# A hybrid encoder layer: the bias table resident, separate buffers for even heads, another layout of v, and smaller rings

## The chip, the cores and the metric

The kernel runs on one core of a Trainium2 chip. The metric is the device time of one execution in microseconds, lower is better, given as the median of several runs. A core has a matrix engine (TensorE; its weight loads are listed apart), VectorE, ScalarE, GpSimd, and a queue engine, SyncE, that here issues nearly all DMAs. On-chip memory (SBUF) has 128 partitions; matmul results land in PSUM banks. Everything else lies in DRAM and comes by DMA.

## The reference

One layer over a sequence of 2048 positions with 1024 channels, in float32, then a final RMSNorm:

```
hn = rmsnorm(x, norm_g)
z  = hn @ w_in                      # one projection, split among three groups of heads
A) attention, 6 heads of 64: scores = q k^T / 8 + rel_bias[clip(distance)], softmax, times v
   over a band of chunks of 64 (own chunk and 8 before); gated by silu(ag)
B) mLSTM, 6 heads of 64: causal conv of width 4 and silu on q and k, chunkwise matrix memory
C) gated linear attention (GLA), 4 heads: chunkwise state with a decay per key channel
out = rmsnorm(x + concat(yA, yB, yC) @ w_out, final_g)
```

The relative bias differs from a constant only in the last 256 key positions of a query tile of 128; the kernel subtracts the constant of far distances and so needs a table of 128 x 6 x 256 for the six heads.

## The kernel before

**Two parts.** The first (from `with ExitStack() as pa_`, line 145) runs four blocks of 512 positions. A block makes all projections, with the mLSTM and GLA work of the block interleaved, and stores what attention needs in DRAM: q (`q_d`), k (`k_d`), v (`v_d`), the gate (`ga_d`), and the finished mLSTM and GLA outputs (`y_d`). The second part (from line 983) loads these, head by head, does attention and the output projection. Six projections of the last block, all for attention, are held back (`kept`) and run as filler between the score steps of attention for block 0 (`proj_kept`, `attention0`, lines 1259 to 1263).

**Precision.** Operands are split in a high and a low part (float32r), and a product takes three matmuls: high x high, high x low, low x high (lines 241 to 243). A weight tile is loaded in `wraw`, its high part cast by ScalarE (line 232), its low part made by VectorE or GpSimd (line 233), into a tile `w` of the ring `wring`, six buffers of 8 KB a partition. A feature projection uses one `w`, and a token projection (`proj_t`, v and part of GLA) holds four through its four position tiles. The second part takes five buffers of the same ring for w_out (line 1025).

**The conv.** `proj_m` runs six projections. Each is copied from its PSUM bank to a tile `u` (ScalarE, line 579); a scale (line 586) and three multiply-adds on VectorE (line 588) read it. `u` has two buffers; the projections use two PSUM banks `ip`. In the last block a tile `u` also holds two GLA outputs (line 911).

**The bias.** `bias_rel` (line 641) runs in the last block: it loads the far constant and, in three pieces, the table, adds the negated constant on ScalarE (line 649), sets masked entries on GpSimd (line 650) and stores the piece in DRAM, `b_d`. The second part loads all of it to `bt` (line 996), 768 KB. VectorE reads `bt` when it takes scores from PSUM (line 1094).

**Heads.** `scores(q, h)` (line 1054) loads for one head of one block the query halves `qq` (two DMAs), the keys `kk` and the values `vv`, the first two from a pool `early` with two buffers each, which lies in the part of SBUF (`side="right"`) that the first part's pools used. It yields between score steps: six for block 0, eight later. `mix(q, h)` transposes the softmax weights, splits them (`ph` on ScalarE, `pl` on VectorE, lines 1144 and 1145) and multiplies by `vv` (lines 1154 and 1157). `attention0` runs heads 0 and 1 with score steps alone, and from head 2 on merges the scores of head h with the mix of head h - 2. `load_wo` (line 1006) loads and splits w_out and the outputs of the first part meanwhile.

**What sets the order.** TensorE runs in program order (`manual_schedule`, line 135). The other engines' and SyncE's orders come from a planner that simulates the program: it takes what is ready by program order, with `high_priority` ahead, and gives buffers out as they come free. `flow` (line 35) decides by estimated times where the mLSTM and GLA steps stand between the projections.

Of the kernel before, what the change touches and what calls it, by code (L numbers as in the profile page):

```python
# [8 lines left out]
FP32 = mybir.dt.float32  # L9
# [7 lines left out]
P = 128  # L17
# [88 lines left out]
def trunk_kernel(ctx: ExitStack, tc: tile.TileContext, xT, x, w_f, w_t, w_o, w_gates, norm_g, conv_w,  # L106
# [9 lines left out]
    v_d = dram.tile([AH, S, P], FP32, name="v_d")  # L116
# [3 lines left out]
    b_d = dram.tile([P, AH, 256], FP32, name="b_d")  # L120

# [19 lines left out]
    wring = pg_.enter_context(tc.tile_pool(name="wring", bufs=6))  # L141
# [3 lines left out]
    with ExitStack() as pa_:  # L145
# [381 lines left out]
        def proj_v(X):  # L527
            vg = big.tile([P, NC, 256], FP32, name="vg", bufs=1)
            vs = []

            def evac1(tt, ps):
                v = ev.tile([P, AH, 2, 64], FR, name="hl")
                v5 = v.rearrange("p (a b) l d -> p a b l d", b=2)
                pv4 = ps[:, 0:384].rearrange("p (a b d) -> p a b d", b=2, d=64)
                nc.scalar.copy(vg[:, tt, P:2 * P], ps[:, 384:512])
                for b in range(2):
                    nc.scalar.copy(v5[:, :, b, b, :], pv4[:, :, b, :])
                    nc.vector.tensor_tensor(v5[:, :, b, 1 - b, :], pv4[:, :, b, :], f32(v5[:, :, b, b, :]), op=ALU.subtract)
                t0 = st["q"] * QT + tt * P
                nc.sync.dma_start(v_d[:, t0:t0 + P, :].rearrange("h t d -> t h d"), f32(v).rearrange("p h l d -> p h (l d)"))  # L540

            def evac0(tt, ps):
                v = big.tile([P, 6, 65], FP32, name="v", bufs=NC)
                vs.append(v)
                nc.scalar.activation(v[:, :, 0:64], ps[:, 0:384].rearrange("p (h d) -> p h d", h=6), AF.Copy, scale=1.0 / 32)
                nc.gpsimd.memset(v[:, :, 64:65], 1.0 / 32)
                nc.scalar.copy(vg[:, tt, 0:P], ps[:, 384:512])  # L547

            proj_t(0, X, evac0)
            yield vs, vg  # L550
            proj_t(1, X, evac1)
            yield
# [19 lines left out]
        def proj_m(X):  # L572
            qk = big.tile([P, 6, QT], FP32, name="qk", bufs=1)
            tail = big.tile([P, 6, 3], FP32, name="tail")
            for b in range(6):
                ps = proj_f(("mq" if b < 3 else "mk") + str(b % 3), X)
                zb = big.tile([P, 3 + QT], FP32, name="u", bufs=2)
# [63 lines left out]
        def bias_rel():  # L641
            bc = big.tile([P, AH], FP32, name="sm")
            nc.sync.dma_start(bc, bias[:, :, 256])
            nc.vector.tensor_scalar(bc, bc, -1.0, None, op0=ALU.mult)
            for p in range(AH // 2):
                b2 = g_tile([P, QT]).rearrange("p (h j) -> p h j", h=2)
                nc.sync.dma_start(b2, bias[:, 2 * p:2 * p + 2, 0:256])
                for h in range(2):
                    nc.scalar.activation(b2[:, h, :], b2[:, h, :], AF.Identity, bias=bc[:, 2 * p + h:2 * p + h + 1])
                nc.gpsimd.memset(b2[0:64, :, 192:256], NEG)  # L650
                nc.sync.dma_start(b_d[:, 2 * p:2 * p + 2, :], b2)
# [191 lines left out]
        def gla(q, vg, gg, G, held=None):  # L843
            for sub in range(2):
# [7 lines left out]
                for c in range(2):  # L852
# [54 lines left out]
                    if held is not None:  # L907
                        if not held:
                            ocs = rows
                        elif len(held) == 2:  # L910
                            ocs = big.tile([P, 3 + QT], FP32, name="u", bufs=2)
# [22 lines left out]
        for q in range(NQ):  # L934
# [3 lines left out]
            if q == NQ - 1:  # L938
# [9 lines left out]
                bias_rel()  # L948
# [21 lines left out]
            flow.need("gates")  # L970
            M = dict(R)
# [12 lines left out]
    with ExitStack() as pb_:  # L984
        psum = pb_.enter_context(tc.tile_pool(name="psumb", bufs=2, space=PSUM, reuse_waits="tile"))
        early = pb_.enter_context(tc.tile_pool(name="early", bufs=2, side="right", reuse_waits="tile"))
# [8 lines left out]
        bt = one.tile([P, AH, 256], FP32, name="bt", bufs=1)  # L995
        nc.sync.dma_start(bt, b_d)
# [57 lines left out]
        def scores(q, h, out_):  # L1054
# [3 lines left out]
            qq = early.tile([P, 2, QT], FR, name="qq")  # L1058
# [4 lines left out]
            kk = early.tile([P, 1024], FR, name="kk")  # L1063
            dma.dma_start(f32(kk[:, :nk]), k_d[h, :, :, kb:kb + nk].rearrange("l d t -> (l d) t"))
            vv = big.tile([P, 8, P], FR, name="vv", bufs=3)
            dma.dma_start(f32(vv[:, :nk // P, :]), v_d[h, kb:kb + nk, :].rearrange("(b p) d -> p b d", p=P))
# [300 lines left out]
```

## Time and profile before

| | |
|---|---|
| runs | median 1308.42 us of 3 (1305.0 to 1312.47) |
| profiled execution | 1308.93 us, of which the span of instructions 1307.2 us |
| mean granted TensorE clock | 0.984 |
| busy | TensorE 1267.8 us, weight loads 1035.1, VectorE 807.6, GpSimd 601.4, ScalarE 592.2 |
| DMA | 179.53 MB in 105937 packets, 137 GB/s on average |

The first part's blocks take about 280, 235, 230 and 162 us; the second part begins at about 907 us. Matmuls are pipelined, so the length of one in the timeline (0.39 us for 128x512) is not its cost: in a row they start 0.23 us apart. A row of the timeline has start, length, engine, line, operation, output and inputs, and in brackets the idle time before it with what ended it. `PEclk` in a table of stretches is the clock that TensorE was granted, 1.00 being full speed. In the list of DMA issues the last number is the median time from issue to landing.

### The profile page before, as it was taken

The page shows a single profiled execution, that of the slowest core. Times are in us where ns is not written, and L with a number is a line of the kernel's source. Part 1 is how long each engine was busy: PE and PEld are TensorE (multiplying, and loading weights), DVE is VectorE, ACT ScalarE, POOL GpSimd, SP SyncE. Part 2 cuts the span into 40 slices and gives each one's busy share as a digit, 9 for nine tenths or more (in the row PEclk, how much of TensorE's full clock was granted, in tenths as well). Part 3 has the DMA queues.
Part 4 walks back from the last instruction along what each step waited for, and adds up shares of the span by engine and source line. Part 5 has one row for each costly group of instructions (what it writes and reads, how often), then busy time and mean ns, then how long its engine had stood idle before and what let it go on. Part 6 is the DMA issues. An engine that isn't in the chain of part 4 may idle for free.

```text
span 1307.2 us, 19535 instructions
## 1 busy us (share of the span) xinstructions
PE 1267.8 (97%) x6924; PEld 1035.1 (79%) x6924; DVE 807.6 (62%) x1866; ACT 592.2 (45%) x1098; POOL 601.4 (46%) x829
## 2 busy tenths in 40 slices
PE   9999999999999999999999999998989989999997
PEld 7777878887787887877778787887777878878876
DVE  6837656762767677276566765653467667666631
ACT  5636322643532246353224643332466556655631
POOL 3337742333765224376523555643164444554432
PEclk8999999999999999998999999999989999999999
DMA  5256234324522442462344332327686565655322
GB/s 201 60 163 228 70 123 135 104 87 148 207 69 94 137 132 57 152 216 85 91 131 123 104 126 64 120 70 234 191 232 212 172 190 160 187 172 180 97 90 80
DMA packets 105937, 179.53 MB, mean 137 GB/s; under 512 B 9712, under 2 KB 54640, under 8 KB 105840
## 3 DMA queue, kind: packets, MB, share of 16 engines
q1 hardware_dynamic: 101376, 170.16, 42.3%
q10 hardware_dynamic: 4464, 8.13, 1.7%
q8 instruction: 54, 0.88, 0.3%
q14 instruction: 43, 0.35, 0.1%
HBM read 141.83 MB, written 36.44 MB: 136 GB/s over the span
## 4 chain that ended last, share of the span: by engine, by line
PE 76%; DVE 7%; POOL 5%; ACT 4%; DMA 4%; issue 3%; SPq 0%; POOLq 0%; ACTq 0%; DVEq 0%
PE ip L241 11%; PE ip L242 10%; PE ip L243 10%; PE ip L1219 4%; PE ip L1221 4%; PE ip L1220 4%; PE ip L261 3%; PE ip L263 3%; PE ip L262 3%; PE s L1078 3%; PE tp L1138 3%; DVE qk L588 2%; PE ga L870 2%; PE w L1154 2%; PE s L722 2%
## 5 line engine op out<-in xcount | busy, mean ns | idle before, releaser
L241 PE MATMUL ip<-x,w 128*128 128x512 f32 x784 | 322.9, 412 | 1.1 <-ACT vg L547 0.8
L243 PE MATMUL ip<-x,w 128*128 128x512 f32 x784 | 308.6, 394 | 0.0
L242 PE MATMUL ip<-x,w 128*128 128x512 f32 x784 | 308.5, 393 | 0.0
L241 PEld LDWEIGHTS ip<-x,w 128*128 128x128 f32 x784 | 148.9, 190 | 42.6 <-issue 12.5
L243 PEld LDWEIGHTS ip<-x,w 128*128 128x128 f32 x784 | 148.7, 190 | 32.7
L242 PEld LDWEIGHTS ip<-x,w 128*128 128x128 f32 x784 | 149.2, 190 | 28.4 <-issue 1.9
L233 POOL TENSOR_TENSOR w<-wraw,w 128x1024 fp32r<-128x1024 f32 x42 | 102.8, 2448 | 117.9 <-ACT w L232 109.3
L232 ACT CAST w<-wraw 128x1024 fp32r<-128x1024 f32 x126 | 131.6, 1046 | 40.7 <-DMA wraw<-in_w_f 24.6
L233 DVE TENSOR_TENSOR w<-wraw,w 128x1024 fp32r<-128x1024 f32 x84 | 114.4, 1363 | 57.6 <-ACT w L232 57.3
L1099 POOL TENSOR_SCALAR pt<-pt,sm 128x640 f32<-128x640 f32 (+2 forms) x96 | 72.1, 752 | 130.2 <-DVE sm L1098 103.1
L261 PE MATMUL ip<-w,x 128*128 128x512 f32 x256 | 102.6, 401 | 3.3 <-ACT vg L547 2.6
L1097 ACT ACTIVATE pt<-pt,sm 128x640 f32<-128x640 f32 (+2 forms) x96 | 73.2, 763 | 63.9 <-DVE sm L1094 60.5
L263 PE MATMUL ip<-w,x 128*128 128x512 f32 x256 | 99.9, 390 | 0.0
L262 PE MATMUL ip<-w,x 128*128 128x512 f32 x256 | 99.7, 390 | 0.0
L1145 DVE TENSOR_TENSOR pl<-tp,ph 128x512 fp32r<-128x512 f32 (+1 forms) x108 | 72.0, 672 | 35.5 <-ACT ph L1144 35.2
L1078 PE MATMUL s<-kk,qq 128*128 128x256 f32 (+2 forms) x360 | 83.6, 317 | 9.2 <-DMA kk<-k_d 5.9
L813 POOL TENSOR_TENSOR prd<-gk,zg 128x16 f32<-128x16 f32 (+7 forms) x112 | 66.0, 589 | 46.2 <-PE pw L819 40.4
L1078 PEld LDWEIGHTS s<-kk,qq 128*128 128x128 f32 x360 | 63.7, 192 | 25.2 <-DVE sm L1094 7.6
L518 ACT ACTIVATE e<-ip 128x512 f32<-128x512 f32 x44 | 26.1, 594 | 120.7 <-PE ip L243 113.5
L1144 ACT CAST ph<-tp 128x512 fp32r<-128x512 f32 (+1 forms) x108 | 60.4, 572 | 41.6 <-PE tp L1138 40.4
L810 POOL TENSOR_TENSOR gk<-gk,al 128x16 f32<-128x16 f32 (+14 forms) x120 | 67.7, 564 | 22.4 <-ACT al L787 14.5
L588 DVE SCALAR_TENSOR_TENSOR qk<-u,cw,qk 128x512 f32<-128x512 f32 x72 | 68.4, 951 | 14.8 <-ACT qk L586 13.4
(362 smaller groups left out, 2534.1 us busy)
## 6 DMA issues: line engine op xcount, KB each, us to landing
wraw<-in_w_f SPq DMA_DIRECT2D x100, 512.0 KB, 3.6
wraw<-in_w_t SPq DMA_DIRECT2D x28, 512.0 KB, 3.8
qq<-q_d SPq DMA_DIRECT2D x48, 256.0 KB, 4.9
kk<-k_d SPq DMA_DIRECT2D x18, 512.0 KB, 6.3
vv<-v_d SPq DMA_DIRECT2D x18, 512.0 KB, 7.1
xraw<-in_xT SPq DMA_DIRECT2D x16, 512.0 KB, 7.1
xr<-in_x SPq DMA_DIRECT2D x16, 512.0 KB, 3.6
out<-xr ACTq DMA_DIRECT2D x31, 256.0 KB, 2.3
```

The lines of the kernel that those rows point to most:

```text
L232: nc.scalar.copy(w[:, :, 0, :], rv)
L233: other().tensor_tensor(w[:, :, 1, :], rv, f32(w[:, :, 0, :]), op=ALU.subtract)
L241: nc.tensor.matmul(ps, w[:, k, 0, :], X[k][:, 0, :], start=(k == 0), stop=False)
L242: nc.tensor.matmul(ps, w[:, k, 0, :], X[k][:, 1, :], start=False, stop=False)
L243: nc.tensor.matmul(ps, w[:, k, 1, :], X[k][:, 0, :], start=False, stop=(k == KT - 1))
L261: nc.tensor.matmul(ps, X[k][:, 0, t], w[:, 0, :], start=(k == 0), stop=False)
L262: nc.tensor.matmul(ps, X[k][:, 0, t], w[:, 1, :], start=False, stop=False)
L263: nc.tensor.matmul(ps, X[k][:, 1, t], w[:, 0, :], start=False, stop=(k == KT - 1))
L588: nc.vector.scalar_tensor_tensor(acc, zb[:, i:i + QT], cw[:, b, i:i + 1], acc, op0=ALU.mult, op1=ALU.add)
L1078: nc.tensor.matmul(sp[:, :cn], qq[:, l, tt * P:(tt + 1) * P], kk[:, ko + c0:ko + c0 + cn], start=(l == 0), stop=(l == 1))
L1097: nc.scalar.activation(pt[:, :n], pt[:, :n], AF.Exp, bias=init, scale=-1.0, accum_out=sm[:, 2:3])
L1099: nc.gpsimd.tensor_scalar(pt[:, :n], pt[:, :n], sm[:, 3:4], 0.5, op0=ALU.mult, op1=ALU.mult)
```

## The change

1. `bt` lies in a pool that lives through the whole kernel. `bias_rel` fills it in one load, six ScalarE operations and one memset, in block 1 in place of block 3; `b_d`, its three stores and the load of the second part are gone.
2. `qq` and `kk` of even heads come from a new pool `early0`, one buffer each, that lives through the whole kernel; those of odd heads from `early`, now with one buffer each. `early` no longer holds `bt`, so it and the pool behind it lie at other addresses.
3. `v_d` is laid out head, partition, block, channel: a head's values for one partition are one run for `vv`'s load, and the store scatters pieces of 512 B at a pitch of 8 KB.
4. `wring` has five buffers, `u` one, and the scratch for software DMAs is 1024 bytes in place of 4096.

```diff
-    v_d = dram.tile([AH, S, P], FP32, name="v_d")
+    v_d = dram.tile([AH, P, S // P, P], FP32, name="v_d")
...
-    b_d = dram.tile([P, AH, 256], FP32, name="b_d")
-
+    bt = const.tile([P, AH, 256], FP32, name="bt")
+    early0 = ctx.enter_context(tc.tile_pool(name="early0", bufs=1))
...
-    wring = pg_.enter_context(tc.tile_pool(name="wring", bufs=6))
+    wring = pg_.enter_context(tc.tile_pool(name="wring", bufs=5))
...
-                nc.sync.dma_start(v_d[:, t0:t0 + P, :].rearrange("h t d -> t h d"), f32(v).rearrange("p h l d -> p h (l d)"))
+                nc.sync.dma_start(v_d[:, :, t0 // P, :].rearrange("h t d -> t h d"), f32(v).rearrange("p h l d -> p h (l d)"))
...
-                zb = big.tile([P, 3 + QT], FP32, name="u", bufs=2)
+                zb = big.tile([P, 3 + QT], FP32, name="u", bufs=1)
...
-            for p in range(AH // 2):
-                b2 = g_tile([P, QT]).rearrange("p (h j) -> p h j", h=2)
-                nc.sync.dma_start(b2, bias[:, 2 * p:2 * p + 2, 0:256])
-                for h in range(2):
-                    nc.scalar.activation(b2[:, h, :], b2[:, h, :], AF.Identity, bias=bc[:, 2 * p + h:2 * p + h + 1])
-                nc.gpsimd.memset(b2[0:64, :, 192:256], NEG)
-                nc.sync.dma_start(b_d[:, 2 * p:2 * p + 2, :], b2)
+            nc.sync.dma_start(bt, bias[:, :, 0:256])
+            for h in range(AH):
+                nc.scalar.activation(bt[:, h, :], bt[:, h, :], AF.Identity, bias=bc[:, h:h + 1])
+            nc.gpsimd.memset(bt[0:64, :, 192:256], NEG)
...
-                            ocs = big.tile([P, 3 + QT], FP32, name="u", bufs=2)
+                            ocs = big.tile([P, 3 + QT], FP32, name="u", bufs=1)
...
-                bias_rel()
                 M = dict(R)
...
             flow.need("gates")
+            if q == 1:
+                bias_rel()
             M = dict(R)
...
-        early = pb_.enter_context(tc.tile_pool(name="early", bufs=2, side="right", reuse_waits="tile"))
+        early = pb_.enter_context(tc.tile_pool(name="early", bufs=1, side="right", reuse_waits="tile"))
...
-        bt = one.tile([P, AH, 256], FP32, name="bt", bufs=1)
-        nc.sync.dma_start(bt, b_d)
...
-            qq = early.tile([P, 2, QT], FR, name="qq")
+            pool = early if h % 2 else early0
+            qq = pool.tile([P, 2, QT], FR, name="qq")
...
-            kk = early.tile([P, 1024], FR, name="kk")
+            kk = pool.tile([P, 1024], FR, name="kk")
...
-            dma.dma_start(f32(vv[:, :nk // P, :]), v_d[h, kb:kb + nk, :].rearrange("(b p) d -> p b d", p=P))
+            dma.dma_start(f32(vv[:, :nk // P, :]), v_d[h, :, kb // P:(kb + nk) // P, :])
...
-    nc = _bacc.Bacc("TRN2", target_bir_lowering=False, num_devices=1, dynamic_dma_scratch_size=4096)
+    nc = _bacc.Bacc("TRN2", target_bir_lowering=False, num_devices=1, dynamic_dma_scratch_size=1024)
```

## The prediction

> **What bounds the kernel now.** I read the page's first part, then the table of stretches, then TensorE's waits.
>
> ```profile
> span 1307.2 us, 19535 instructions
> PE 1267.8 (97%) x6924; PEld 1035.1 (79%) x6924; DVE 807.6 (62%) x1866; ACT 592.2 (45%) x1098; POOL 601.4 (46%) x829
> ```
>
> TensorE has work in flight for 1267.8 of 1307.2 us; no other engine passes 62%. No part of the change takes a matmul away, so all it can win is the 39.4 us in which TensorE stands idle and the time in which its clock is lowered. Where are they?
>
> ```profile
> 280.00:515.00 235.00, 231.31 (x1262) 186.34 (x1261) 150.34 (x290) 95.42 (x163) 108.57 (x157) 0.99 0.39 122
> 515.00:745.00 230.00, 226.88 (x1232) 182.44 (x1231) 137.93 (x283) 94.12 (x165) 110.11 (x167) 0.99 0.42 130
> 745.00:907.00 162.00, 160.95 (x940) 130.79 (x938) 95.26 (x204) 58.52 (x103) 80.87 (x121) 1.00 0.36 113
> 907.00:1000.00 93.00, 80.62 (x406) 66.93 (x406) 55.40 (x168) 49.83 (x114) 40.91 (x45) 0.91 0.81 234
> ```
>
> The columns are stretch, length, busy time of TensorE, its weight loads, VectorE, ScalarE and GpSimd, granted clock, DMA share, GB/s. Blocks 1 and 2 of the first part lose 3.7 and 3.1 us, block 3 loses 1.1. The passage from the projections to attention (907 to 1000) loses 12.4 us, and there the clock is 0.91 and the DMA engines are 81% busy. TensorE's wait list and timeline name the two largest single stops of the passage:
>
> ```profile
> PE s L1078 <- DMA kk<-k_d: 5.9, 2, 3.0
> ...
> 910.09 0.66 PE L1078 MATMUL s<-kk,qq 128*128 128x128 f32 x2 [2.98 <-DMA kk<-k_d]
> ...
> 925.82 0.41 PE L1078 MATMUL s<-kk,qq 128*128 128x128 f32 x2 [2.94 <-DMA kk<-k_d]
> ```
>
> Both wait for keys: those of head 0, and 16 us later those of head 2. Behind each stop the clock is down, as the stretch table has it:
>
> ```profile
> 910.00:915.00 5.00, 4.91 (x19) 4.24 (x20) 1.39 (x9) 1.10 (x4) 1.32 (x3) 0.68 1.09 362
> ...
> 925.00:930.00 5.00, 4.18 (x16) 3.64 (x17) 1.46 (x5) 1.08 (x3) 0.37 (x1) 0.68 0.61 169
> ```
>
> **The change, part by part.**
>
> *Even heads' own buffers.* SyncE's queue shows why head 0's keys are late:
>
> ```profile
> 897.27 1.03 SPq L996 DMA_DIRECT2D bt<-b_d  x1
> 898.35 0.61 SPq L1061 DMA_DIRECT2D qq<-q_d  x1
> ...
> 900.45 0.62 SPq L1064 DMA_DIRECT2D kk<-k_d  x1
> ...
> 906.34 0.33 SPq L1064 DMA_DIRECT2D kk<-k_d  x1
> ...
> 916.65 1.89 SPq L1061 DMA_DIRECT2D qq<-q_d  x2
> 918.58 0.60 SPq L1064 DMA_DIRECT2D kk<-k_d  x1
> ```
>
> The buffers of heads 0 and 1 lie on memory that the first part still uses, so nothing of theirs goes out before 897; head 0's keys are issued at 900.45 and used at 910.09, 9.6 us later, behind the bias table and others on DMA engines that are already full. With memory of its own, head 0's two query halves and its keys can be issued once block 0 has stored them. Three issues of some 0.6 us each leave SyncE's crowded stretch. The first stop goes: 2.98 us, and the clock loss behind it, (1 - 0.68) x 5 = 1.6 us. Sum **4.6 us**. What lies ready instead: the score banks, and the bias table, resident now. Next late could be head 1, whose odd buffer still lies on the old memory; its keys were issued at 906.34 behind a store, and that store stood still for the bias table:
>
> ```profile
> SPq L616 <- DMA bt<-b_d: 2.6, 1, 2.6
> ...
> qq<-q_d SPq DMA_DIRECT2D x48, 256.0 KB, 4.9
> kk<-k_d SPq DMA_DIRECT2D x18, 512.0 KB, 6.3
> vv<-v_d SPq DMA_DIRECT2D x18, 512.0 KB, 7.1
> v_d<-hl SPq DMA_DIRECT2D x16, 384.0 KB, 3.1
> kk<-k_d SPq DMA_DIRECT2D x6, 256.0 KB, 6.5
> vv<-v_d SPq DMA_DIRECT2D x6, 256.0 KB, 6.2
> bt<-b_d SPq DMA_DIRECT2D x1, 768.0 KB, 8.4
> ```
>
> Without the table and without head 0's loads ahead of it, head 1's keys can go out at about 901; 6.5 us makes 907.5, and head 0's six score steps keep TensorE until 912.5. So no new stop there.
>
> The second stop is less certain. Head 2 uses head 0's buffer before and after: it was refilled as soon as head 0's last score ended (issue 916.65), and its keys arrived at 925.8. Afterwards head 0 ends about 4.6 us earlier and TensorE wants head 2 six steps of head 1 later, about 6 us. Before, issue to use took 925.82 - 916.65 = 9.2 us. What shrinks this is the queue in front of it: 768 KB of bias table and head 0's 2 x 256 + 256 KB, 1.5 MB together, no longer move in this stretch. At the 362 GB/s of the fullest row that is 4.3 us, and 9.2 - 4.3 = 4.9, under the 6. The bounds are a wait that stays (gain 0) and one that goes, 2.94 + (1 - 0.68) x 5 = 4.5 us. With only 1 us of margin I leave **1.0 us** of it standing and take **3.5 us**.
>
> The Trainium skill's page "TensorE: Matmul & The Clock Gate", in the table of "Why this matters for your kernels", allows idle gaps up to about 3 us before the clock drops. By that rule neither stop would cost clock, and the two would be worth 2.98 + 2.94 = 5.9 us instead of 9.1. The trace disagrees: the clock is 0.68 behind gaps of 2.98 and 2.94 us, and by that I go.
>
> *Bias kept on chip.* The store to and the load from DRAM go (three stores and one load of SyncE, 768 KB each way), and the six ScalarE operations move from block 3 to block 1, with one wide load instead of three.
>
> ```profile
> L649 ACT ACTIVATE g<-g,sm 128x256 f32<-128x256 f32 x6 | 2.7, 501 | 0.5 <-DMA g<-in_bias 0.4
> ```
>
> That is 6 x 0.50 = 3.0 us of ScalarE in block 1, where it is busy 95.42 of 235 us; GpSimd's one memset is smaller still, and nothing reads the result before attention. Price 0; without that cover it would be 3.0 us and the memset. What the missing load frees is counted above.
>
> *v in rows.* A head's v becomes one run of 4 KB a partition instead of eight of 512 B. Keys of the same size, already in runs, land in 6.3 us against 7.1; at 256 KB it is 6.5 against 6.2. So a load gains between 0 and 0.8 us, and TensorE's list has no wait for v. The stores keep their 512 B pieces but scatter them. They land in 3.1 us now, and the pair of buffers comes round only every two tiles, 11 us (a projection's 5.4 us twice, below), so they could take three times as long unseen. Price 0 both ways.
>
> The skill's "DMA: Bandwidth & Descriptors", under "Specifications", has full rate from 512 B on, so the layout would win nothing; the two pairs of rows point both ways and cannot decide, and the sum holds 0.
>
> *Five w buffers.* The tightest place is block 1, where the first value projection holds four:
>
> ```profile
> 261.06 1.05 ACT L232 CAST w<-wraw 128x1024 fp32r<-128x1024 f32 x1
> ...
> 278.86 0.39 PE L263 MATMUL ip<-w,x 128*128 128x512 f32 x1
> ...
> 284.24 0.39 PE L241 MATMUL ip<-x,w 128*128 128x512 f32 x1
> ...
> 289.68 0.39 PE L241 MATMUL ip<-x,w 128*128 128x512 f32 x1
> ...
> L233 POOL TENSOR_TENSOR w<-wraw,w 128x1024 fp32r<-128x1024 f32 x42 | 102.8, 2448 | 117.9 <-ACT w L232 109.3
> ```
>
> The cast now made at 261.06 must wait until the first of the four is done at 279.25. With 1.05 and at worst 2.45 us it is ready at 282.8, and TensorE wants it at 289.68, after the projection that begins at 284.24 (5.4 us): 6.9 us spare. Price 0; if other work of ScalarE and GpSimd took more than that, TensorE would stop by the difference.
>
> *One u buffer.* This is the added wait. The copy of a conv input (L579) must now wait for the last of the three conv steps (L588) of the one before.
>
> ```profile
> 332.05 0.57 ACT L579 COPY u<-ip 128x512 f32<-128x512 f32 x1
> 335.02 0.58 ACT L579 COPY u<-ip 128x512 f32<-128x512 f32 x1
> ...
> 339.67 1.41 DVE L588 SCALAR_TENSOR_TENSOR qk<-u,cw,qk 128x512 f32<-128x512 f32 x2
> ...
> 340.71 0.39 PE L241 MATMUL ip<-x,w 128*128 128x512 f32 x1
> ...
> L588 DVE SCALAR_TENSOR_TENSOR qk<-u,cw,qk 128x512 f32<-128x512 f32 x72 | 68.4, 951 | 14.8 <-ACT qk L586 13.4
> L586 ACT ACTIVATE qk<-u,cw 128x512 f32<-128x512 f32 x24 | 17.3, 719 | 0.2
> ```
>
> A chain of copy, scale and three conv steps is 0.57 + 0.72 + 3 x 0.95 = 4.1 us bare; the one that begins at 332.05 lasts until 340.4 (the first of the pair at 339.67 ends it), 8.4 us. A projection takes TensorE 5.4 us. So six chains in a row add lag only if they average over 5.4, and the two PSUM banks forgive one projection less a copy, 4.9 us; over five follow-ups TensorE stops where the mean passes 5.4 + 4.9 / 5 = 6.4. The middle of 4.1 and 8.4 is 6.3, just below. The copy at 335.02 would move to 340.5 and end 0.4 us after 340.71, when TensorE wants that bank. Behind a waiting copy stand, in ScalarE's order, the scale of the same tile and casts of w, which have the spare time above. I take **+0.5 us**; ends 0 and, with a mean chain of 7.0, 5 x 1.6 - 4.9 = 3.1 us and 1.6 of clock in each of four blocks, 19 us.
>
> *Order.* ScalarE, VectorE, GpSimd and SyncE are ordered anew by the planner. Blocks of the same program lose 3.7, 3.1 and 1.1 us now, a spread of 2.6; I allow 5 us either way and take 0.
>
> *Sum.* The profiled execution has 1308.9 us, 1.7 beside its span: 1308.9 - 4.6 - 3.5 + 0.5 = 1301.3. The median of the runs, 1308.4, lies 0.5 lower, so **1301** is predicted.
>
> **The rivals.**
>
> *Only the first stop goes.* Head 2 still takes over head 0's buffer, and 9.2 us from issue to use is longer than head 1's 6. Against it: 1.5 MB less in front. 1308.9 - 4.6 + 0.5 = 1304.8.
>
> *The single u buffer decides.* If the chains of L579 to L588 average over 6.4 us, TensorE stops at the next bank. For it: the chain of 8.4 us, and this row, where TensorE waits for such a copy already:
>
> ```profile
> 347.19 0.50 PE L241 MATMUL ip<-x,w 128*128 128x512 f32 x1 [0.30 <-ACT u L579]
> ```
>
> Against it: bare chains of 4.1. At a mean of 7.0 it is 1308.9 - 8.1 + 19 = 1319.8, slower; at 6.7 it is still 4 x (5 x 1.3 - 4.9 + 1.6) = 13 us, 1313.8, no change.
>
> *The later stops go too.* Between 965 and 975 TensorE waits for the pieces of the softmax weights while ScalarE and VectorE split w_out:
>
> ```profile
> 966.74 0.49 PE L1154 MATMUL w<-ph,vv 128*128 128x512 f32 x1 [1.10 <-ACT ph L1144]
> 974.29 0.33 PE L1157 MATMUL w<-pl,vv 128*64 128x256 f32 x1 [2.17 <-DVE pl L1145]
> ```
>
> If the emptier DMA queue lets w_out come early, 3.3 us and two cold spells, at 1.6 as above, go: 1301.3 - 6.5 = 1294.8. Against it: the splits move up with TensorE, and so does what they collide with.
>
> *The early load isn't early.* The planner may still issue head 0's loads in program order behind the last stores; then only the bias load is gone, which the stop may outlast: 1308.9 + 0.5 = 1309.4.
>
> **How the numbers follow.** Forecast 0.40, first stop only 0.22, u buffer 0.17, later stops too 0.15, not early 0.06. No change within 0.5%, about what a measurement of this kernel can tell, reaches from 1301.9 to 1315. The forecast's own range is 1296 to 1306; of its 0.40 I put 0.25 under 1301.9. Faster: 0.25 + 0.15 + 0.04 of the second = 0.44. Slower: 0.15 of the u case, 0.02 of the last = 0.17. Same: 0.39. The range for 8 in 10 goes from 1292, below the case with the later stops, to 1313, which leaves out most of the u case.
>
> **What would show it.** Right: the loads of qq and kk for head 0 long before 890 in SyncE's queue, no TensorE wait for kk at the first score, a clock near 1.00 just behind it, the passage at 6 us idle or less. Head 2's share: whether the one wait for kk that may remain is under 1 us. Wrong: TensorE rows on L241 that wait for ACT u L579 in each block; waits for w; or a passage whose 8 us come back between 960 and 1000.

## The result, and the profile after

The changed kernel takes 1305.35 us (median of 16 executions, 1301.96 to 1310.75); the kernel before takes 1309.85 us beside it. The ratio is 0.9969, 95% interval 0.9954 to 0.9984: about 4 us or 0.3% faster, which lies inside the 0.5% that the prediction counts as no change, and is a little over half of the forecast gain (1301 was predicted, against 1308.4). The profiled execution has a span of 1304.1 us against 1307.2.

The first part of the page, after:

```profile
span 1304.1 us, 19554 instructions
PE 1265.2 (97%) x6924; PEld 1030.5 (79%) x6924; DVE 803.0 (62%) x1866; ACT 592.4 (45%) x1098; POOL 601.6 (46%) x827
```

TensorE's idle time is 1304.1 - 1265.2 = 38.9 us; it was 39.4. So hardly any idle time has gone. Where did it move? Here is the table of stretches, first the rows of before that the prediction did not show, then after; the columns are those of the prediction (stretch, length, busy time of TensorE, weight loads, VectorE, ScalarE, GpSimd, granted clock, DMA share, GB/s).

```profile
0.00:80.00 80.00, 75.66 (x346) 61.83 (x347) 54.41 (x125) 44.00 (x66) 29.52 (x49) 0.94 0.42 138
80.00:280.00 200.00, 200.00 (x1125) 161.15 (x1124) 129.44 (x274) 86.42 (x149) 99.48 (x153) 1.00 0.39 125
```

```profile
0.00:80.00 80.00, 73.20 (x325) 59.39 (x326) 51.99 (x122) 42.91 (x64) 30.43 (x49) 0.91 0.38 128
80.00:280.00 200.00, 197.67 (x1107) 157.95 (x1106) 126.68 (x253) 83.27 (x144) 97.62 (x142) 1.00 0.42 134
280.00:515.00 235.00, 232.16 (x1272) 187.46 (x1273) 141.87 (x297) 97.25 (x170) 109.45 (x163) 1.00 0.38 121
...
907.00:1000.00 93.00, 84.44 (x439) 69.40 (x438) 55.84 (x174) 52.71 (x118) 40.85 (x46) 0.94 0.78 234
```

The passage (907 to 1000) idles 8.6 us instead of 12.4, and its clock is 0.94 instead of 0.91: the part of the change that was forecast to win did win. But the first 80 us idle 2.5 us more (6.8 against 4.3) and the next 200 us 2.3 us more (2.3 against 0). The first part gave back in idle time what the passage won.

In the passage the rows are those that the prediction asked for. (The line numbers in a row are those of its own kernel; the same statement stands a few lines higher or lower in another.) Head 0's query and key loads now stand in SyncE's queue some 690 us before they are used, head 2's follow at the old place:

```profile
188.60 0.62 SPq L1058 DMA_DIRECT2D qq<-q_d  x1
...
217.55 0.34 SPq L1061 DMA_DIRECT2D kk<-k_d  x1
...
910.82 0.33 PE L1075 MATMUL s<-kk,qq 128*128 128x128 f32 x2
...
915.91 1.23 SPq L1058 DMA_DIRECT2D qq<-q_d  x2
917.20 1.28 SPq L1061 DMA_DIRECT2D kk<-k_d  x1
...
923.25 0.41 PE L1075 MATMUL s<-kk,qq 128*128 128x128 f32 x2 [1.10 <-DMA kk<-k_d]
```

Head 0's first score (at 910.82) has no wait any more, and head 2's has 1.10 us where it had 2.94.

In the first part there are two new places. At 62 to 79 us, in block 0, TensorE waits three times in a row, for 4.0 us in all; before, in the first fence, it waits there for 0.80 and 0.73 us:

```profile
61.95 0.50 PE L241 MATMUL ip<-x,w 128*128 128x512 f32 x1 [0.80 <-ACT vg L547]
...
68.89 0.50 PE L261 MATMUL ip<-w,x 128*128 128x512 f32 x1 [0.73 <-DVE e L524]
```

```profile
64.73 0.50 PE L243 MATMUL ip<-x,w 128*128 128x512 f32 x1 [1.15 <-DVE w L233]
72.56 0.50 PE L261 MATMUL ip<-w,x 128*128 128x512 f32 x1 [2.10 <-DVE e L524]
...
77.99 0.50 PE L262 MATMUL ip<-w,x 128*128 128x512 f32 x1 [0.79 <-POOL w L233]
```

And in block 1, where the bias work now is, TensorE stands for 2.58 us. The timeline of ScalarE, VectorE, SyncE and TensorE at that place:

```profile
271.31 0.60 SPq L643 DMA_DIRECT2D sm<-in_bias  x1
...
275.94 0.53 ACT L743 ACTIVATE m<-m 128x384 f32<-128x384 f32 x1
279.15 0.91 ACT L647 ACTIVATE bt<-bt,sm 128x256 f32<-128x256 f32 x2 [2.69 <-DVE sm L644]
279.97 0.47 ACT L545 ACTIVATE v<-ip 128x384 f32<-128x384 f32 x1
...
278.50 0.54 DVE L745 TENSOR_REDUCE sm<-m 128x6 f32<-128x384 f32 x1
278.96 0.15 DVE L644 TENSOR_SCALAR sm<-sm 128x6 f32<-128x6 f32 x1
...
280.64 0.50 PE L261 MATMUL ip<-w,x 128*128 128x512 f32 x1 [2.58 <-ACT vg L547]
```

Read from below: TensorE needs the bank that L545 and L547 empty. ScalarE has been free since 276.5, but the next instruction in its order is the bias operation L647, and that one waits for L644, the 0.15 us negation of six numbers, which stands in VectorE's order behind other work until 278.96. The load of those six numbers was issued at 271.31 and landed 3.6 us later, so by 275 the data was there.

**Idle time and clock.** The executions of either kernel differ by some 10 us, and most of that goes with the granted clock. Over 218 executions of the kernels of this study, compared within each kernel, 0.001 of mean granted clock is worth 0.95 us (correlation 0.85); two more, of 1553 and 2068 us at a mean clock of 0.775 and 0.554, are left out here and in the ratios. So each time can be split, as an estimate: 1 us for each 0.001 that the clock lacks, and the rest, which is work and idle time at full clock. Within a profile the granted clock has two values only, 1.00 and 0.50; the second is called half clock below.

| kernel | executions | mean time | mean clock | at full clock |
|---|---|---|---|---|
| before | 87 | 1311.3 | 0.9852 | 1296.5 ± 0.3 |
| after | 28 | 1305.9 | 0.9907 | 1296.6 ± 0.5 |

(± is the 95% interval of the mean.) By this split the two kernels take the same time at full clock; all that the change wins is clock, 5.5 us of it. The forecast had 4.9 us of idle time (2.98 + 2.94 - 1.0) and 3.2 us of clock.

### The profile page after: what moved, and what is told of

It is laid out like the page before. It is cut to its first block, busy times and chain, and to the rows that moved or that the text cites. A ratio compares the mean times of both kernels' runs of the same rounds, so it can differ in the third digit from the quotient of the medians.

```text
span 1304.1 us, 19554 instructions
## 1 busy us (share of the span) xinstructions
PE 1265.2 (97%) x6924; PEld 1030.5 (79%) x6924; DVE 803.0 (62%) x1866; ACT 592.4 (45%) x1098; POOL 601.6 (46%) x827
## 4 chain that ended last, share of the span: by engine, by line
PE 73%; DVE 9%; DMA 5%; POOL 5%; ACT 4%; issue 4%; SPq 0%; POOLq 0%; DVEq 0%; ACTq 0%
PE ip L241 10%; PE ip L243 10%; PE ip L242 10%; PE ip L1216 4%; PE ip L1218 4%; PE ip L1217 4%; PE s L1075 3%; PE ip L261 3%; PE ip L262 3%; PE ip L263 3%; PE tp L1135 3%; DVE qk L588 2%; PE ga L867 2%; PE w L1154 2%; PE w L1151 2%
## 5 line engine op out<-in xcount | busy, mean ns | idle before, releaser
L241 PEld LDWEIGHTS ip<-x,w 128*128 128x128 f32 x784 | 147.3, 188 | 41.4 <-issue 12.0
L243 PEld LDWEIGHTS ip<-x,w 128*128 128x128 f32 x784 | 147.2, 188 | 34.2 <-DVE w L233 1.6
L242 PEld LDWEIGHTS ip<-x,w 128*128 128x128 f32 x784 | 147.6, 188 | 28.1 <-issue 1.7
L588 DVE SCALAR_TENSOR_TENSOR qk<-u,cw,qk 128x512 f32<-128x512 f32 x72 | 71.2, 990 | 20.2 <-ACT qk L586 18.8
L807 POOL TENSOR_TENSOR gk<-gk,al 128x16 f32<-128x16 f32 (+14 forms) x120 | 71.5, 596 | 23.1 <-ACT al L784 15.8
```

Of the source, the lines that this page charges most:

```text
L241: nc.tensor.matmul(ps, w[:, k, 0, :], X[k][:, 0, :], start=(k == 0), stop=False)
L242: nc.tensor.matmul(ps, w[:, k, 0, :], X[k][:, 1, :], start=False, stop=False)
L243: nc.tensor.matmul(ps, w[:, k, 1, :], X[k][:, 0, :], start=False, stop=(k == KT - 1))
L588: nc.vector.scalar_tensor_tensor(acc, zb[:, i:i + QT], cw[:, b, i:i + 1], acc, op0=ALU.mult, op1=ALU.add)
```

## The experiments

All ratios are against the kernel before, run on the same chip beside them. "After" stands for the changed kernel. A table at the end sets the profiles side by side.

**The far constant early.** The six numbers are loaded and negated with the other constants at the start; the rest of the bias work stays in block 1.

```
# load_consts: bc in a buffer of its own
+ nc.sync.dma_start(bc, bias[:, :, 256])
+ nc.vector.tensor_scalar(bc, bc, -1.0, None, op0=ALU.mult)
# bias_rel (block 1): these two lines go
```

> The changed kernel, but the far constant of the bias (a load of 3 KB and its negation) is fetched with the other small constants at the start, into a tile of its own; the six bias operations stay in block 1. Theory (the bias operations stand at the head of ScalarE's order and wait for this small load, and TensorE waits for the copy behind them, 2.58 us at L261 before 280 us): that stop goes, no TensorE wait of over 1 us between 270 and 290 us, and the time falls by 2 to 3 us against the changed kernel, to some 0.995 of before. Rival (the stop comes from the planner's order with five w buffers, the bias only happens to stand there): the stop stays within 1 us of its place and the time stays at 0.997.

Measured: 1304.44 us, ratio 0.9943 (0.9922 to 0.9965). ScalarE empties the value tile where it waited before, and no TensorE row between 270 and 283 has an idle time:

```profile
273.58 0.53 ACT L743 ACTIVATE m<-m 128x384 f32<-128x384 f32 x1
274.02 0.48 ACT L548 ACTIVATE v<-ip 128x384 f32<-128x384 f32 x1
274.39 0.26 ACT L550 COPY vg<-ip 128x128 f32<-128x128 f32 x1
...
352.22 0.50 PE L244 MATMUL ip<-x,w 128*128 128x512 f32 x1 [1.10 <-ACT u L582]
```

So the stop at 278 is the bias work in ScalarE's order, held by the negation. Of its 2.6 us some 0.7 came back 70 us later, in a wait for a conv input's copy (1.10 us, where after has 0.42). Against after the kernel wins 2.1 us at full clock (interval 0.4 to 3.7).

**Without the own buffers.** After, but heads 0 to 5 share two buffers as before; the bias table stays on chip.

```
- pool = early if h % 2 else early0
+ pool = early            # early: bufs=2, no early0
```

> The changed kernel without the even heads' own buffers: all heads from one pool of two, on memory that the first part uses, as before; bias table resident, v in rows, five w and one u stay. Theory (own buffers carry the passage's gain): a wait for kk of 2 to 3 us before head 0's first score comes back with its cold clock, likely head 2's too, 5 to 8 us more than the changed kernel, so 1.000 to 1.003 of before. Rival (the gain came from the bias table's load being out of the queue): no wait over 1 us at head 0, and the time stays at 0.997.

Measured: 1310.91 us, ratio 1.0000 (0.9980 to 1.0019). The whole gain is gone. But head 0 does not wait; head 2 does, and longer than in either of the two kernels:

```profile
917.99 0.56 SPq L1061 DMA_DIRECT2D kk<-k_d  x1
...
927.34 0.59 PE L1075 MATMUL s<-kk,qq 128*128 128x128 f32 x2 [4.97 <-DMA kk<-k_d]
```

With the table's load out of the way, head 0's keys come in time even from the shared buffer. Head 2's keys are issued at 917.99, against 918.58 before; TensorE, no longer stopped at head 0, comes to head 2 earlier and waits there instead. At full clock this kernel takes 1300.1 ± 0.6 us, 3.5 more than after. Two kernels below with the passage of before show the same trade in their profiles: 0.87 us at head 0 and 5.98 at head 2 with one u buffer, 1.94 and 3.79 with the copy of dr moved. The two stops are not two prices to be added: the second is set by a time of arrival, and takes up what the first gives.

**Five w buffers alone**, in the kernel before:

```
- name="wring", bufs=6
+ name="wring", bufs=5
```

> The kernel before with five w buffers in place of six and nothing else. Theory (the fifth buffer's lack makes the casts of block 0 late): TensorE rows at L241 to L243 and L261 to L263 that wait for L233 or L524 between 60 and 80 us, together 3 to 4 us against 1.5 before, and the time 1.5 to 3.5 us over before (1.001 to 1.003). Rival (block 0's new waits come from the planner's order of the whole change): no more waits there than before, time 1.000.

Measured: 1310.82 us, ratio 0.9994 (0.9978 to 1.0010), the time of the kernel before. The rows of block 0 are those of the changed kernel to 0.1 us:

```profile
64.67 0.50 PE L243 MATMUL ip<-x,w 128*128 128x512 f32 x1 [1.17 <-DVE w L233]
72.44 0.50 PE L261 MATMUL ip<-w,x 128*128 128x512 f32 x1 [2.04 <-DVE e L524]
```

So the missing sixth buffer makes these waits: each of the nine profiles with five buffers has a stop of 1.15 to 1.19 us for w at 62 to 65 us, and none of the five with six has one. At full clock this kernel takes 1299.6 ± 1.2, 3.1 us more than before; its mean clock, 0.9889, gives 3.7 us back. In its profile two places where TensorE stands just long enough before to lose its clock (353 and 593, below) cost no clock.

**One u buffer alone**, in the kernel before:

```
- name="u", bufs=2
+ name="u", bufs=1
```

> The kernel before with one change alone: one u buffer instead of two. Theory (the wait is real but small: in the trace after, TensorE's L241 waits on ACT u in two gaps of 0.39 and 0.42 us): 0.5 to 1 us above the kernel before, ratio 1.000 to 1.001. Rival (the single buffer is the cause of the first part's 3.7 us): 3 us or more above it, ratio 1.0025 or more, with L241 rows that wait on ACT u in each of the four blocks.

Measured: 1305.11 us, ratio 0.9955 (0.9938 to 0.9972): neither expectation. This one edit makes the kernel as fast as the whole change does. At full clock it takes 1295.3 ± 2.1, before 1296.5: the work and the idle time are the same within the interval, and 5.0 of the 6.2 us between the means are clock, 0.9902 against 0.9852. One of the places, where TensorE waits for the copy of dr; before in the first fence, one u buffer in the second, each with the stretches of 3.4 us around it from the table of stretches:

```profile
355.10 0.33 PE L866 MATMUL gb<-ident,dr 128*128 128x128 f32 x1 [2.18 <-ACT dr L823]
...
353.38:356.79 3.41, 1.69 (x16) 1.69 (x16) 2.67 (x4) 2.29 (x4) 2.83 (x6) 1.00 0.03 11
356.79:360.21 3.42, 3.42 (x11) 2.75 (x11) 2.62 (x4) 1.87 (x3) 3.03 (x10) 0.50 0.47 153
```

```profile
356.89 0.33 PE L866 MATMUL gb<-ident,dr 128*128 128x128 f32 x1 [0.79 <-ACT dr L823]
...
355.90:359.31 3.41, 2.62 (x20) 2.34 (x20) 3.03 (x5) 1.56 (x4) 3.10 (x7) 1.00 0.48 150
```

The stop is 1.4 us shorter, and no half clock follows it. At the other place, 594, the stop is 0.70 us where before has 1.74, with the same outcome.

**The bias part undone.** After, but the table is worked out in block 3, stored and loaded back as before.

```
# q == 3 again, in place of q == 1:
+ bias_rel()          # three loads, six ScalarE operations, three stores to b_d
# start of attention
+ nc.sync.dma_start(bt, b_d)
```

> The kernel after with the bias part undone: the far constant is subtracted in block 3, the table is stored to DRAM and loaded back at the start of attention; own buffers, v in rows, one u and five w stay. Theory (the move costs 2.8 us in block 1; the missing load of 768 KB is worth about as much at head 2, where the wait for keys grows from 1.1 to 3 or 4 us): 1304 to 1307, no difference from the kernel after that can be measured. Rival (with own buffers the load is hidden anyway): the stop of 2.6 us at 278 goes and nothing comes back, 1301 to 1303.

Measured: 1307.06 us, ratio 0.9963 (0.9946 to 0.9980), not to be told from after. The theory's two halves are both there: no stop between 270 and 280, and head 2 waits three times as long.

```profile
926.46 0.66 PE L1079 MATMUL s<-kk,qq 128*128 128x128 f32 x2 [3.32 <-DMA kk<-k_d]
```

Keeping the bias on chip costs 2.6 us in block 1 and wins something at head 2, where after has 1.10 us (1.85 in a second profile, below). How much can't be read from single profiles, because the stop at head 2 varies: 2.94, 3.79, 5.98 and 6.21 us in four kernels with the same passage (before, the copy of dr moved, one u, five w). In the time the two cancel: at full clock this kernel takes 1296.1 ± 0.7, after 1296.6 ± 0.5.

**The layout of v undone.** After, with v stored and loaded as before.

```
- v_d[h, :, kb // P:(kb + nk) // P, :]
+ v_d[h, kb:kb + nk, :].rearrange("(b p) d -> p b d", p=P)
```

> The kernel after with the old layout of v (eight pieces of 512 B a partition instead of one run of 4 KB). Theory (TensorE waits nowhere for v): within 1 us of the kernel after, 1304.5 to 1306.5; a load of v lands in 7.1 us again instead of 6.4. Rival (v's loads lie in front of head 2's keys, and longer runs are what made room for them): head 2's wait for keys grows from 1.1 to about 2 us with a cold spell behind it, 1307 to 1309.

Measured: 1307.31 us, ratio 0.9971 (0.9951 to 0.9991). The median lies in the rival's range, but the difference from after is not clear of noise (1.2 ± 2.1 us between the means, 0.4 ± 1.2 at full clock). In the profile the rival's row is there: a load of v lands in 7.2 us again (after 6.4 and, in its second profile, 6.8), and the keys of head 2, on the same DMA engines, are used 9.2 us after the first issue for head 2 (923.45 - 914.26), where after has 7.3 and 8.1.

```profile
vv<-v_d SPq DMA_DIRECT2D x18, 512.0 KB, 7.2
...
923.45 0.41 PE L1075 MATMUL s<-kk,qq 128*128 128x128 f32 x2 [2.96 <-DMA kk<-k_d]
```

A second profile of after (below) has 1.85 us at this place where the first has 1.10, so of the 1.9 us between 1.10 and 2.96 a part is chance. Whether the layout wins a microsecond stays open.

**An own buffer for head 0 of block 0 alone**, two shared buffers for all other heads, the far constant early; with two u buffers and with one.

```
+ first = q == 0 and h == 0
+ pool = early0 if first else early        # early: bufs=2
+ kk = pool.tile([P, QT if first else 1024], FR, name="kk")
# first kernel also: name="u", bufs=2
```

> The changed kernel with the extra pool cut to head 0 of block 0 alone (4 KB of queries, 2 KB of keys), all other heads from a pool of two as before; the far constant fetched at the start as in e1; the freed memory gives u its second buffer back. Theory: head 2 no longer refills head 0's buffer, so its wait for kk (1.10 us) goes as well; with the bias stop (2.6) and the waits for u (0.8) gone the time is 4 to 6 us under the changed kernel, 0.992 to 0.994 of before. Rival (heads 1 and 2, both on the first part's memory, now compete for the full DMA engines, and head 1 comes late): a wait for kk at head 1 of over 1 us and no gain over e1.

> As the version with an own buffer for head 0 of block 0 alone, two buffers for all others and the far constant loaded at the start, but with one u buffer. Theory (the second u buffer is worth the two gaps of 0.4 us): 0.5 to 1 us above that version, 1298 to 1299 where the kernel before takes 1310. Rival (the second u buffer is what gives that version its lead): 1301 to 1303.

Measured: 1297.57 us, ratio 0.9906 (0.9881 to 0.9931), and with one u buffer 1301.49, ratio 0.9924 (0.9906 to 0.9942). Neither has a wait for keys at heads 0, 1 or 2: head 2 no longer needs the buffer that head 0 is using, and its loads go out with head 1's. The stretch of the passage, with two u buffers:

```profile
907.00:1000.00 93.00, 83.11 (x461) 68.51 (x460) 62.52 (x192) 56.84 (x127) 45.23 (x51) 1.00 0.73 228
```

At full clock the two take 1290.8 ± 1.6 and 1291.3 ± 1.5: in work and idle time no difference can be told. Of the 2.7 us between the means, themselves hardly clear of noise, 2.2 are clock (0.9923 and 0.9902): the rival's number came, in the main by clock. How little decides about that shows at one place where both stand idle for 1.7 us ahead of the same matmul (the rows are one stretch of 3.41 us with the stop, and the next):

```profile
363.08:366.49 3.41, 1.70 (x8) 1.12 (x7) 3.41 (x8) 1.26 (x5) 1.75 (x4) 1.00 0.47 137
366.49:369.90 3.41, 3.41 (x27) 2.84 (x26) 2.69 (x10) 1.74 (x3) 0.00 (x0) 1.00 0.06 22
```

```profile
365.56:368.97 3.41, 1.71 (x12) 1.24 (x10) 3.41 (x10) 0.51 (x2) 0.98 (x4) 1.00 0.52 159
368.97:372.39 3.42, 3.42 (x18) 2.56 (x17) 2.63 (x8) 2.52 (x4) 0.18 (x1) 0.51 0.00 0
```

With two u buffers (first fence) the clock stays, with one (second) it halves for the next 3.4 us. TensorE is busy for half of the stretch in both.

**Matmuls in place of the wait.** The kernel before, with nine matmuls of ones with ones ahead of the first score of heads 0 and 2 (the profile counts two for each).

```
+ for _ in range(9 if q == 0 and tt == 0 and h in (0, 2) else 0):
+     nc.tensor.matmul(sp[:, 0:P], ones, ones, start=True, stop=True)
```

> The kernel before with nothing of the change: ahead of the first score of heads 0 and 2 in block 0, nine matmuls of ones with ones write the bank that the score overwrites, some 2.1 us of TensorE work in place of waiting for keys; the result is the reference's. Theory (the clock falls for 3.4 us behind every fixed stretch of 3.41 us in which TensorE was busy for less than about half, so a stop of 2.98 us costs clock besides its own length, in most executions): the stops for keys shrink to under 1 us, no half clock at 910 and 927, mean clock up by about 0.002, 2 to 3 us under the kernel before. Rival (a stop under 3.4 us costs its own length alone): the clock at 910 and 927 and the time stay as they are, within 1 us of the kernel before.

Measured: 1314.02 us, ratio 1.0011 (0.9989 to 1.0033). No gain, against the theory.

```profile
911.36 2.17 PE L1077 MATMUL s<-ones 128*128 128x128 f32 x18
914.06 0.41 PE L1079 MATMUL s<-kk,qq 128*128 128x128 f32 x2 [0.53 <-DMA kk<-k_d]
...
925.26 2.17 PE L1077 MATMUL s<-ones 128*128 128x128 f32 x18
931.49 0.50 PE L1079 MATMUL s<-kk,qq 128*128 128x128 f32 x2 [4.05 <-DMA kk<-k_d]
```

At head 0 the clock indeed stays (no half clock until 931), and TensorE needs 11.2 us from head 0's first score to head 2's (914.06 to 925.26) where it needed 12.8 (910.09 to 922.88). But head 2's loads still go out only when head 0's last score is done (at 921.03, 7.0 us after its first; before 6.6), and TensorE waits there for 2.17 + 4.05 us, with a half clock behind it. The clock saved ahead of this wait for a DMA is spent in the wait.

**After once more**, unchanged:

> The changed kernel once more, beside the others of this call. Theory (where the fixed 3.41 us stretches fall against the kernel differs from one execution to the next): the idle rows of TensorE are those of its first profile to 0.1 us, but the half-clock stretches lie elsewhere, at the start 6.8 or 10.2 us instead of 13.7, and at 62 to 78 us one may stand. Rival (the clock belongs to the program): the same half-clock stretches at the same places. Time 1304 to 1307 either way.

Measured: 1306.28 us, ratio 0.9966 (0.9943 to 0.9989). The large stops of the first 910 us are the same (here those at 72 and 280), those of the passage are not:

```profile
72.58 0.50 PE L261 MATMUL ip<-w,x 128*128 128x512 f32 x1 [2.16 <-DVE e L524]
...
280.61 0.50 PE L261 MATMUL ip<-w,x 128*128 128x512 f32 x1 [2.58 <-ACT vg L547]
...
924.05 0.47 PE L1075 MATMUL s<-kk,qq 128*128 128x128 f32 x2 [1.85 <-DMA kk<-k_d]
```

The half clock at the start lasts 13.7 us again, so the theory missed there; in the passage it lies at 924, where the first profile had none.

**The copy of dr on VectorE**, in the kernel before:

```
- nc.scalar.copy(dr, dr_ps[:, 0:ST])
+ nc.vector.tensor_copy(dr, dr_ps[:, 0:ST])
```

> The kernel before with one instruction moved: the copy of dr (L823) on VectorE instead of ScalarE. Theory (the stop of 2.18 us at 352.9 is this copy standing in ScalarE's queue behind a tanh that waits 4.0 us for the conv steps and behind a cast; that stop, and not any work saved, is what the changed kernel and the one with one u buffer win there): the stop goes or falls under 0.5 us and, with its clock, 2 to 4 us at 356; 1307.5 to 1309.5 where the kernel before takes 1311. Rival (the stop only moves: the copy waits behind the conv steps on VectorE): the stop stays over 1.5 us, 1311.

Measured: 1308.66 us, ratio 0.9983 (0.9964 to 1.0001), an interval that still holds no change. The stop at L866 goes from 2.18 to 1.57 us, and half clock still follows it (357.2 to 360.6); the copy waits on VectorE nearly as it waited on ScalarE, as the rival has it.

```profile
356.14 0.33 PE L866 MATMUL gb<-ident,dr 128*128 128x128 f32 x1 [1.57 <-DVE dr L823]
```

**The least part of the change.** The kernel before with an own buffer for head 0 of block 0, and one u buffer (and a smaller scratch for DMA descriptors) to make room for it. Bias, v and w are as before.

```
+ first = q == 0 and h == 0
+ pool = early0 if first else early        # early: bufs=2
- name="u", bufs=2
+ name="u", bufs=1
```

> The kernel before with the least part of the change: an own buffer for head 0 of block 0 alone (keys of 512 columns), one u buffer to make room; the bias table still goes through DRAM, v keeps its old layout, w keeps six buffers, all other heads keep two shared buffers. Theory (what the change wins is the early load of head 0 and, where the second buffer stays, of head 2; the resident bias table and v in rows are not needed, and five w buffers and the bias work in block 1 cost 2 to 3 us each): no stop for keys over 1 us at heads 0 to 2, no stop of 2.6 us at 278, 1297 to 1300 where the kernel before takes 1311. Rival (the table's 768 KB in the passage hold up the keys that now go out with it): stops of 2 to 4 us at head 1 or 2, 1302 to 1305.

Measured: 1296.79 us, ratio 0.9892 (0.9868 to 0.9915), the fastest of all: 15 us under the kernel before and about 9 under the changed one. At full clock it takes 1288.4 ± 1.2; one u buffer alone takes 1295.3 there, so head 0's own buffer is worth some 7 of the 8.1 us won there.

```profile
214.35 0.34 SPq L1066 DMA_DIRECT2D kk<-k_d  x1
...
80.00:280.00 200.00, 199.53 (x1121) 160.32 (x1120) 128.65 (x271) 84.96 (x146) 96.03 (x151) 1.00 0.41 131
...
907.00:1000.00 93.00, 86.12 (x470) 70.76 (x469) 62.63 (x189) 56.40 (x126) 44.04 (x51) 0.98 0.79 236
```

The passage idles 6.9 us, less than with any other kernel, although the table's 768 KB are loaded in it, and no score of heads 0 to 2 waits for keys. The version above with one u buffer differs from this kernel in five w, the bias and v; it takes 2.9 us more at full clock (interval 1.2 to 4.6).

**Side by side.** TensorE's matmuls are the same, in the same order, in all these kernels (the nine of ones apart), so the same two matmuls bound a part in each. The projections run from the 96th matmul (about 24 us) to the last one ahead of head 0's first score; the passage from there to the 5301st, about 90 us later. Each from one profile: length, idle time of TensorE, time at half clock.

| kernel | projections: length, idle, half clock | passage: length, idle, half clock |
|---|---|---|
| before | 883.9, 9.4, 10.2 | 92.5, 12.4, 17.1 |
| one u | 879.5, 8.2, 0 | 91.9, 14.5, 10.2 |
| five w | 883.7, 12.2, 0 | 94.6, 16.1, 13.7 |
| after, bias as before | 888.8, 10.9, 13.7 | 89.4, 10.8, 13.7 |
| after | 885.7, 13.3, 0 | 86.3, 8.6, 10.2 |
| after, second profile | 885.8, 13.7, 0 | 89.0, 10.2, 13.7 |
| after without own buffers | 886.2, 14.2, 0 | 92.3, 14.1, 10.2 |
| head 0 alone, constant early, two u | 882.2, 10.8, 0 | 83.0, 9.9, 0 |
| least part | 879.3, 8.6, 0 | 82.0, 6.9, 3.4 |

In the idle time of the projections the parts add up: 9.4 - 1.2 (one u) + 2.8 (five w) + 2.4 (bias: after less after with the bias as before) = 13.4, and after has 13.3. What does not add up is the half clock, which comes and goes with stops near 1.7 us.

## Why the prediction was right or wrong

*The passage* was right in kind and near in size. The first stop is gone, the second is 1.10 us where 1.0 was left standing. The matmul order lets the passage be measured as a whole: 92.5 us before, 86.3 and 89.0 us in two profiles after, a gain of 6.3 or 3.5 us (from the unrounded times) against a forecast of 8.1. But the two stops were priced as two sums. Taking the own buffers away again, and filling the first stop with other work, both showed that head 2's stop takes up what is won at head 0. The emptier DMA queue alone (no own buffers) leaves 4.97 us of the 5.92 us of both stops, the own buffers alone (bias part undone) leave 3.32, and both together 1.10 or 1.85: only together do they come near what the two prices said.

*The time from issue to use of head 2's keys* was estimated at 9.2 - 4.3 = 4.9 us, by dividing the 1.5 MB that no longer move there by 362 GB/s. It measured 923.25 - 915.91 = 7.3 us, and 924.05 - 915.96 = 8.1 us in the second profile. Taking the bytes away bought 1.8 or 1.1 us, not 4.3. The margin of 1 us that was laid on top covered it by luck: TensorE came to head 2 at 922.15, 6.2 us after the issue.

*Bias kept on chip, priced 0*, was wrong, and it is one of the two steps that failed. The cover named for it, ScalarE busy for 95 of 235 us, was a share of a stretch. What counted was the order: six operations that nothing needs before attention stand ahead of the emptying of a PSUM bank that TensorE needs at once, and the first waits for a negation that comes late in VectorE's order. The prediction counted six operations and a memset and left out the 0.15 us negation, which set the time. The bound it gave for lost cover, 3.0 us, is above the 2.4 to 2.6 us found. That the time hardly shows this loss is because the missing load, counted in another term, wins about as much.

*Five w buffers, priced 0*, is the other. The working looked for the tightest place in block 1 and found 6.9 us to spare there; block 1 has no wait for w, before or after. The waits came in block 0, at 62 to 79 us, which was not looked at. Five w buffers alone cost 3.1 us at full clock. The list of "what would show it" had "waits for w" among the signs of a wrong forecast, and they are there.

*One u buffer* was priced at 0.5 us, with a rival that made it 13 to 19. No chain of waits forms: with one u buffer TensorE waits for such a copy once in block 1, for 0.2 to 1.2 us, in two profiles also for 0.1 us in block 0, and not in the other blocks. In idle time it costs nothing that can be told (-1.2 us in the projections, 1295.3 ± 2.1 against 1296.5 at full clock). That the kernel with this change alone is 6 us faster is in the main clock, which no step of the prediction had: "Order: I allow 5 us either way and take 0" is where it belongs, and its size was right for either sign.

*v in rows*: loads of v land 0.7 us sooner in one profile and 0.3 in the other, inside the bounds, and in the time no gain can be told from noise.

*The clock.* The Trainium skill's page "TensorE: Matmul & The Clock Gate" was cited for gaps up to about 3 us that cost no clock, and the trace was taken against it. The traces agree with that choice: half clock follows the stop of 2.18 us at 355 in before, and one of 1.57 us at the same place with the copy of dr moved. But the prediction took a cold spell behind every stop as certain, and had no term for the three half-clock stretches that before has in the projections (357 to 360 and 596 to 603, in the prediction only a clock of 0.99 in two rows). They went without any part of the change aiming at them. What they cost: TensorE works 883.9 - 9.4 = 874.5 us there before, and 870.7 to 872.4 us in the kernels of the table without half clock, so 2 to 4 us.

So the sum that would have met the profiled execution is 1308.9 - 6.3 in the passage + 2.8 for w + 2.4 for the bias - 1.2 for u - 2.1 for the clock in the projections + 2.0 ahead of the 96th matmul, where half clock lasted 13.7 us instead of 10.2, - 0.7 behind the passage = 1305.8; it has 1305.85. Two losses of together 5 us were missing, and a windfall of clock hid part of them.

## What to carry to other kernels

A cover is an order, not a share: for each operation that is moved onto an engine, name what stands right behind it in that engine's order, and follow its smallest input (here six numbers) back through the queue it comes from. A stop that waits for a transfer's arrival takes up whatever is won ahead of it, so two stops on one chain aren't added, and the transfer is issued earlier instead, which here one small buffer did alone; the memory for more of it was paid for with a ring buffer whose tight place was elsewhere than the one looked at. Where executions differ by their granted clock, compare at full clock first, and ask of every stop whether it is just above or just below what halves the clock.

## What the runs showed of the hardware that was not expected

The granted clock is set in fixed stretches of 3.41 us. In each of the 14 profiles all falls to half clock lie on one such grid (in that of before, 264 stretches between the falls at 8.6 and 909.8 us), whose position against the kernel differs from execution to execution, and from 25 us on the share of the stretch just ended in which TensorE was busy nearly decides:

| busy share of a stretch at full clock | stretches | half clock in the next |
|---|---|---|
| under 0.40 | 26 | 26 |
| 0.40 to 0.50 | 21 | 15 |
| 0.50 to 0.58 | 37 | 8 |
| 0.58 to 0.65 | 24 | 0 |
| over 0.65 | 4963 | 0 |

So idle time of under 1.4 us in one stretch cost only itself, and over about 1.7 us (a share under 0.50) it cost the next 3.4 us at half clock in 41 of 47 stretches; a longer stop can escape if the grid cuts it in two. The stop of 2.58 us in block 1 of the changed kernel did, in its profile (the rows are two stretches of its grid, to 0.1 us):

```profile
275.90:279.35 3.45, 2.16 (x10) 1.47 (x8) 3.31 (x13) 0.74 (x3) 1.44 (x4) 1.00 0.01 2
279.35:282.80 3.45, 2.16 (x9) 1.80 (x10) 3.35 (x16) 3.42 (x9) 0.69 (x3) 1.00 0.00 0
```

What decides between 0.40 and 0.58 is not shown, and the first fall of each profile doesn't fit: in before it comes at 8.65 us behind a stretch with a share of 0.78, filled in part by matmuls one column wide.

The Trainium skill's page "TensorE: Matmul & The Clock Gate", under "What's actually happening", has a free-running window of 3413 ns and says that the clock falls after an idle one; the grid agrees, 901.2 / 264 = 3.41 us, and the runs add that half idle is enough. Where the grid falls is the likely reason why executions of one kernel lie 10 us apart: their times go with the granted clock, but only one execution per run has a profile that would show the grid. An edit that saves no work, such as the one u buffer, was worth 6 us; in its profile two stops had become short enough to cost no clock.
